# Hybrid encoder on one core: the projection phase's background work put out by a VectorE time budget, one chain step per block

## The chip, the cores and the metric

One Trainium2 chip, one core of it. The time is device microseconds of one execution. A median of three runs is given for the kernel before; the trace is of one further execution.

## The reference

One encoder layer and a last normalisation, for two request groups (prompt and sample) of 2048 tokens and 1024 channels each, with the same weights. One projection makes every branch's input:

```python
h = rmsnorm(x, norm_g)
p = h @ w_in
hy_u, hy_z, cf_a, cf_z, xa_q, xa_z = jnp.split(p, SPLITS, axis=-1)
k2 = hyena_two_sided_filter(L, ...)
y_hy = hyena_branch(hy_u, hy_short_w, hy_short_b, k2, hy_skip) * jax.nn.silu(hy_z)
y_cf = conformer_branch(cf_a, cf_dw_w, cf_dw_b, cf_ln_g, cf_ln_b) * jax.nn.silu(cf_z)
y_xa = memory_attention(xa_q, rmsnorm(mem, mem_norm_g), xa_w_kv) * jax.nn.silu(xa_z)
mix = jnp.concatenate([y_hy, y_cf, y_xa], axis=-1)
return x + mix @ w_out
```

`conformer_branch` is a gated value, a depthwise convolution of 31 taps over positions, a layer norm over 256 channels and a silu. `hyena_two_sided_filter` is three small layers with sines, an output matmul and a decay. `hyena_branch` is a convolution of width 3 on three projections, and a long convolution by Fourier transforms. All of it in float32.

## The kernel before

Matmuls of float32 data are made from three products of a high and a low part (`split`, L178 and L179: a cast on ScalarE, a subtraction on POOL or, for some, VectorE). The kernel has a **projection phase**, up to about 1381 us, then attention and the Fourier transforms, then the output phase. The change touches the first.

The projection has 26 weight columns of 128 channels for each of the two groups, and four token blocks of 512: 208 **blocks** of 24 matmuls (8 pieces of the depth, 3 products, L416 to L418, `proj`). Blocks 0 to 103 are group 0, 104 to 207 group 1. A block writes one of two PSUM banks (`pj`), and ScalarE's copy or activation, for Q also a VectorE subtraction (L522, L523), reads it and frees it. Column order in a group: CG and CV (gate and value of the conformer), ZC, then X1 and V in turn (blocks 24 to 55, in group 1 128 to 159), ZH and X0 in turn (56 to 87, 160 to 191), then ZX and Q. Blocks of X1, V and X0 pass the short convolution: a ScalarE copy (L430), POOL's middle tap (L437), VectorE's two others (L439, L441); V also a POOL product (L458).

In the shadow of these blocks runs **background** work, in two queues of closures, `bgq` and `fq`. After each block a number of closures is popped and run (L678): 7 a column from `bgq`, one from `fq`. What is run there is put into the program at that place; the Tile scheduler then orders each engine's instructions by a timeline of its own. The queues are filled at given columns (`QUEUE`, L628):

- the memory's keys and values (`kv_background`), after the first chunk of columns;
- the conformer's convolution for each group (`cf_background`): for each of four token blocks (b0 to b3 in group 0, b4 to b7 in group 1) a start on POOL, 60 taps on VectorE (L220: 30 more taps, two halves of the channels), then a chain: the mean of the two halves (POOL sum L226, split, two matmuls with a matrix of ones L228 and L229), subtraction (L235), squares (L240), their mean by the same lines, Sqrt (L242), reciprocal on VectorE (L245), a product and a silu (L249, L250), a product with the gate and the store (L256);
- the Hyena filter (`filter_background`, from block 102 on): for each of eight pieces three layers (`mlp`: matmul L295, VectorE L297, POOL, VectorE L303 three times, POOL, sine L306) and four times `taps` (matmuls L321 to L323, VectorE product L326, matmul L333, store);
- the first steps of the Fourier transforms of group 0 (`a_background`): load, transposes (L607), matmuls (L614 to L616).

What is left in the queues is put out behind the last block (`bg(len(fq), fq)`, `bg(len(bgq))`).

## Time and profile before

| what | value |
|---|---|
| median of three runs | 2147.4 us (2142.19 to 2153.81) |
| the profiled execution | 2152.26 us |
| its span | 2150.5 us |
| PE busy | 2008.1 us |
| VectorE busy | 1281.9 us |
| mean granted clock of TensorE | 0.978 |
| end of the projection phase | 1380.5 us |

The span is what the profiler saw from the first to the last instruction. A window row gives for a stretch the busy time of each engine with its count of instructions, and the granted TensorE clock (1.00 is 2.4 GHz, 0.50 is 1.2 GHz). A wait row tells which engine and line waited for which, in total, how often and the longest.

### The profile page before, as it was taken

What the parts mean: (1) busy time and instruction counts of PE and PEld (TensorE: products, weight loads), DVE (VectorE), ACT (ScalarE), POOL (GpSimd) and SP (SyncE); (2) the same over time, 40 slices, a digit from 0 to 9 for tenths busy, and PEclk for the clock granted to TensorE, in tenths of its full rate; (3) what the DMA queues carried; (4) which work ended last, traced back from release to release, by engine and by line L of the source; (5) the groups of instructions that cost most, each with busy time, mean ns of one, the idle gap of its engine ahead of it and who ended that gap; (6) DMA issues with size and microseconds to landing.
All of it is one profiled execution on the core that took longest, in us unless ns stands there. A gap on an engine that the chain in (4) does not pass through costs nothing.

```text
span 2150.5 us, 26677 instructions
## 1 busy us (share of the span) xinstructions
PE 2008.1 (93%) x9186; PEld 1603.0 (75%) x9186; DVE 1281.9 (60%) x1779; ACT 777.1 (36%) x1475; POOL 905.5 (42%) x861
## 2 busy tenths in 40 slices
PE   5999998987999999999999899999998789999998
PEld 4888876776787788877777678789733278888886
DVE  5756397978316363479495952277897724333443
ACT  5531212131424233232333243377787711111211
POOL 3434475655433111465554541365598811111110
PEclk8999999999999999999999999999999999999999
DMA  9643222331656332222222237799688776655552
GB/s 331 206 171 133 88 99 89 108 109 69 225 180 221 125 108 100 80 92 73 103 81 102 93 106 225 210 296 270 194 263 266 236 196 153 155 148 151 145 152 57
DMA packets 198306, 333.95 MB, mean 155 GB/s; under 512 B 53161, under 2 KB 74297, under 8 KB 195354
## 3 DMA queue, kind: packets, MB, share of 16 engines
q1 hardware_dynamic: 170938, 273.11, 41.0%
q10 hardware_dynamic: 21392, 46.18, 6.5%
q0 software_dynamic: 5840, 12.95, 2.2%
q8 instruction: 73, 1.20, 0.2%
q14 instruction: 63, 0.52, 0.1%
HBM read 200.50 MB, written 131.66 MB: 154 GB/s over the span
## 4 chain that ended last, share of the span: by engine, by line
PE 63%; DVE 16%; DMA 9%; issue 5%; POOL 3%; ACT 3%; SPq 1%; ACTq 0%; POOLq 0%; DVEq 0%
PE pj L417 11%; PE pj L418 11%; PE pj L416 11%; DVE bg L220 9%; PE ms L943 5%; PE ms L945 5%; PE ms L944 5%; PE tr L926 2%; PE po L767 2%; DVE sm L439 2%; DMA in<-xf 2%; PE pa L819 1%; DVE big L367 1%; PE ms L553 1%; PE ms L746 1%
## 5 line engine op out<-in xcount | busy, mean ns | idle before, releaser
L416 PE MATMUL pj<-xh,whi 128*128 128x512 f32 (+1 forms) x1728 | 672.0, 389 | 29.2 <-ACT xh L386 8.7
L417 PE MATMUL pj<-xl,whi 128*128 128x512 f32 (+1 forms) x1728 | 670.6, 388 | 8.0 <-POOL xl L387 6.7
L418 PE MATMUL pj<-xh,wlo 128*128 128x512 f32 (+1 forms) x1728 | 669.2, 387 | 0.0
L220 DVE SCALAR_TENSOR_TENSOR bg<-bg,vb,bg 128x512 f32<-128x512 f32 x480 | 418.0, 903 | 10.5 <-POOL bg L215 5.7
L416 PEld LDWEIGHTS pj<-xh,whi 128*128 128x128 f32 x1728 | 331.8, 192 | 99.4 <-ACT xh L386 9.6
L417 PEld LDWEIGHTS pj<-xl,whi 128*128 128x128 f32 x1728 | 332.1, 192 | 73.0 <-POOL xl L387 7.7
L418 PEld LDWEIGHTS pj<-xh,wlo 128*128 128x128 f32 x1728 | 332.3, 192 | 64.9 <-DMA wlo<-ws 0.4
L943 PE MATMUL ms<-wo,mh 128*128 128x512 f32 x512 | 205.9, 402 | 1.8 <-ACT mh L178 1.8
L944 PE MATMUL ms<-wo,mh 128*128 128x512 f32 x512 | 200.5, 392 | 0.0
L945 PE MATMUL ms<-wo,ml 128*128 128x512 f32 x512 | 198.4, 394 | 0.2 <-POOL ml L179 0.2
L439 DVE SCALAR_TENSOR_TENSOR sm<-sm,va,sm 128x448 f32<-128x448 f32 (+1 forms) x96 | 83.7, 871 | 162.7 <-POOL sm L437 133.4
L437 POOL TENSOR_SCALAR sm<-sm,va 128x448 f32<-128x448 f32 (+1 forms) x96 | 113.3, 1180 | 136.9 <-ACT sm L430 130.4
L458 POOL TENSOR_TENSOR big<-big,sm 128x448 f32<-128x448 f32 (+1 forms) x64 | 121.2, 1894 | 107.9 <-DVE sm L441 101.2
L946 DVE TENSOR_TENSOR xr<-xr,ms 128x512 f32<-128x512 f32 x64 | 44.0, 688 | 202.9 <-PE ms L945 202.9
L185 POOL TENSOR_TENSOR ss<-ss,mhalf 128x1 f32<-128x1 f32 x32 | 17.6, 550 | 315.9 <-DVE ss L184 315.9
L183 ACT ACTIVATE junk<-xr 128x1024 bf16<-128x1024 f32 x32 | 33.8, 1058 | 318.4 <-DVE xr L946 318.4
L430 ACT COPY sm<-pj 128x512 f32<-128x512 f32 x96 | 56.2, 585 | 213.9 <-PE pj L418 167.9
L179 POOL TENSOR_TENSOR wlo<-sm,whi 128x512 fp32r<-128x512 f32 x50 | 82.1, 1658 | 72.4 <-ACT whi L178 62.1
L943 PEld LDWEIGHTS ms<-wo,mh 128*128 128x128 f32 x512 | 96.8, 189 | 20.5 <-ACT mh L178 2.6
L945 PEld LDWEIGHTS ms<-wo,ml 128*128 128x128 f32 x512 | 96.1, 188 | 20.9 <-POOL ml L179 0.6
L944 PEld LDWEIGHTS ms<-wo,mh 128*128 128x128 f32 x512 | 96.7, 189 | 18.9
L758 POOL TENSOR_TENSOR ynp<-ynp,se 128x512 f32<-128x512 f32 x64 | 66.0, 1040 | 63.0 <-DVE se L756 53.7
(179 smaller groups left out, 3061.1 us busy)
## 6 DMA issues: line engine op xcount, KB each, us to landing
big<-in_xt_dram SPq DMA_DIRECT2D x32, 512.0 KB, 5.7
in<-x1d SPq DMA_DIRECT2D x128, 128.0 KB, 3.3
aa<-o ACTq DMA_DIRECT2D x64, 256.0 KB, 3.0
at<-aa SPq DMA_DIRECT2D x64, 256.0 KB, 4.1
out_dram<-xr ACTq DMA_DIRECT2D x64, 256.0 KB, 3.2
sm<-in_win_dram SPq DMA_DIRECT2D x52, 256.0 KB, 3.3
ws<-whi SPq DMA_DIRECT2D x52, 256.0 KB, 2.2
ws<-wlo SPq DMA_DIRECT2D x52, 256.0 KB, 4.1
```

The source lines that it names most:

```text
L179: (sub_eng or nc.gpsimd).tensor_tensor(lo, src, hi.bitcast(F32), op=ALU.subtract)
L220: nc.vector.scalar_tensor_tensor(st["a", c], st["h", c][:, k:k + TB], vb[:, 2 * k + c:2 * k + c + 1], st["a", c], op0=ALU.mult, op1=ALU.add)
L416: nc.tensor.matmul(ps[:, ts_], hi, xh[:, k, ts_], start=k == 0, stop=False)
L417: nc.tensor.matmul(ps[:, ts_], hi, xl[:, k, ts_], start=False, stop=False)
L418: nc.tensor.matmul(ps[:, ts_], lo, xh[:, k, ts_], start=False, stop=k == KC - 1)
L437: nc.gpsimd.tensor_scalar(ct[:, o:e], pt[:, o + 1:e + 1], w[1], va[:, 52 + ch:53 + ch], op0=ALU.mult, op1=ALU.add)
L439: nc.vector.scalar_tensor_tensor(ct[:, o:e], pt[:, o:e], w[0], ct[:, o:e], op0=ALU.mult, op1=ALU.add)
L458: nc.gpsimd.tensor_tensor(v, v, out, op=ALU.mult)
L758: nc.gpsimd.tensor_tensor(ev, ev, se.unsqueeze(2).broadcast_to([P, 2, 256]), op=ALU.mult)
L943: nc.tensor.matmul(po, mh[:, k, :], woh[k][:, hs], start=i == 0, stop=False)
L944: nc.tensor.matmul(po, mh[:, k, :], wol[k][:, hs], start=False, stop=False)
L945: nc.tensor.matmul(po, ml[:, k, :], woh[k][:, hs], start=False, stop=i == 7)
```

## The change

Every closure gets a cost in VectorE microseconds and a mark that says whether it belongs to a chain. After each block, `background(us)` gets a credit of 6.0 us less the VectorE time of the block's own column (2.2 for X0, X1 and V, 0.8 for CV and Q, 0.1 for others), and runs closures from `fq`, then `bgq`, while the credit is above zero. A marked closure runs only in a block in which its queue has put out nothing else.

```diff
-    LEAD, BR, FR, PF = 8, 7, 1.0, 0
+    LEAD, PF = 8, 0
...
-    def bg(n, q=bgq):
-        for _ in range(min(n, len(q))):
-            q.popleft()()
+    pace = {"block": 0, "credit": 0.0, "last": {id(bgq): -1, id(fq): -1}}
+
+    def background(us):
+
+        pace["block"] += 1
+        pace["credit"] = min(pace["credit"], us) + us
+        chained = set()
+        while pace["credit"] > 0:
+            for q in (fq, bgq):
+                if not q:
+                    continue
+                cost, chain, fn = q[0]
+                if chain and (id(q) in chained or pace["last"][id(q)] == pace["block"]):
+                    continue
+                if chain:
+                    chained.add(id(q))
+                q.popleft()
+                fn()
+                pace["last"][id(q)] = pace["block"]
+                pace["credit"] -= cost
+                break
+            else:
+                break
...
-                        background(BR * len(cs), FR)
+                        background(sum(6.0 - own(col) for col, _ in cs))
```

The conformer's chain is cut into other steps: the sum and its split (`total`); mean, subtraction, squares, their sum and split (`center`); the second mean, Sqrt, reciprocal and products (`var`); silu, gate and store (`outp`). Before they were mean with sum, split and subtraction; squares with sum, split and Sqrt; reciprocal; products and silus; gate and store, all by the rate of 7.

```diff
+            def halves(st, src, tmp):
+                st["hi"], st["lo"] = bt(TB, F32R), bt(TB, F32R)
                 nc.gpsimd.tensor_tensor(tmp, src[0], src[1], op=ALU.add)
-                split(hi, lo, tmp)
...
+                        bgq.append((0.9, False, lambda st=st, c=c, k=k: tap(st, c, k)))
+                bgq.append((0.5, True, lambda st=st: total(st)))
+                bgq.append((1.4, True, lambda st=st: center(st)))
+                bgq.append((3.4, True, lambda st=st: var(st)))
+                bgq.append((0.0, True, lambda st=st, b=b: (outp(st, b, 0), outp(st, b, 1))))
```

In the filter, the second matmul of `taps` (`spec`) comes one step later, and the layers of the next piece stand between the taps of this one:

```diff
-            for b in range(8):
-                st = {}
-                for ly in range(3):
-                    fq.append(lambda st=st, b=b, ly=ly: mlp(st, b, ly))
-                for n in range(4):
-                    fq.append(lambda st=st, b=b, n=n: taps(st, b, n))
+            for b in range(8):
                 for n in range(4):
+                    def step(b=b, n=n):
+                        if b or n:
+                            spec(b - (n == 0), (n - 1) % 4)
+                        taps(b, n)
+                        if b < 7 and n:
+                            mlp(st, b + 1, n - 1)
+                    fq.append((3.2 if b < 7 and n else 0.8, True, step))
```

The steps of keys and values and of `a_background` are marked as chains (costs 4.5, 1.3, 4.0 and 0.7); the two matmul steps after one transpose are one closure now.

Three places of the instruction order follow. PE around the first mean of token block b1 of the conformer, `ms` its PSUM tile, `pj` the block's; of before, where L228 is the mean's high part:

```order
L416 MATMUL pj_2815<-xh_786,whi_2520 128x512
L417 MATMUL pj_2815<-xl_787,whi_2520 128x512
L228 MATMUL ms_2602<-bg_2603,ones 128x512
L418 MATMUL pj_2815<-xh_786,wlo_2521 128x512
L416 MATMUL pj_2815<-xh_786,whi_2520 128x512
```

and of the change, where L256 and L257 are the two parts and L456 to L458 the block:

```order
L458 MATMUL pj_3018<-xh_608,wlo_2810 128x512
L256 MATMUL ms_3051<-bg_3013,ones 128x512
L257 MATMUL ms_3051<-bg_3014,ones 128x512
L456 MATMUL pj_3063<-xh_786,whi_2801 128x512
L457 MATMUL pj_3063<-xl_787,whi_2801 128x512
```

The mean stood within block 47, 17 matmuls in; it now stands between blocks 54 and 55, both parts together. PE at the end of block 200, in the change (b7, the last of group 1; L654 to L656 and L647 are matmuls and transposes of `a_background`):

```order
L458 MATMUL pj_9498<-xh_4816,wlo_9364 128x512
L256 MATMUL ms_9135<-bg_9097,ones 128x512
L257 MATMUL ms_9135<-bg_9098,ones 128x512
L256 MATMUL ms_9182<-bg_9142,ones 128x512
L257 MATMUL ms_9182<-bg_9143,ones 128x512
L654 MATMUL ms_9442<-bg_9405,big_9356 128x512
L655 MATMUL ms_9442<-bg_9405,big_9356 128x512
```

Both means of b7 stand back to back there, and nine more rows of `a_background` follow before block 201; before, the first mean stood behind block 191 and the second 14 matmuls into block 193. VectorE around the reciprocal of b7, before:

```order
L235 TENSOR_TENSOR bg_7675<-bg_7675,ms_8158 128x512
L439 SCALAR_TENSOR_TENSOR sm_9191<-sm_9187,va,sm_9191 128x576
L303 SCALAR_TENSOR_TENSOR f_8107<-f_8062,f_8107 128x256
L441 SCALAR_TENSOR_TENSOR sm_9191<-sm_9187,va,sm_9191 128x576
L303 SCALAR_TENSOR_TENSOR f_8107<-f_8062,f_8107 128x256 x2
L245 RECIPROCAL bg_7669<-bg_7669 128x512
L326 TENSOR_TENSOR f_8186<-ms_8182,f_8186 128x512
```

and in the change (L266 is the subtraction, L275 the reciprocal, L658 and L204 a copy and a split of `a_background`, L563 the subtraction that reads Q's PSUM bank, here of block 199):

```order
L266 TENSOR_TENSOR bg_8702<-bg_8702,ms_9135 128x512
L266 TENSOR_TENSOR bg_8706<-bg_8706,ms_9135 128x512
L204 TENSOR_TENSOR bg_9406<-tr_9400,bg_9405 128x512
L275 RECIPROCAL bg_8700<-bg_8700 128x512
L658 COPY sm_9446<-ms_9442 128x512
L204 TENSOR_TENSOR bg_9495<-tr_9489,bg_9494 128x512
L563 SCALAR_TENSOR_TENSOR sm_9482<-pj_9456,sm_9481 128x512
```

Before, the reciprocal was followed by the filter's product; now a read of a projection bank comes after it.

## Rows read from the trace of the kernel before

**Rows 1.** Page: busy us (share of the span) and instructions of each engine.

```profile
PE 2008.1 (93%) x9186; PEld 1603.0 (75%) x9186; DVE 1281.9 (60%) x1779; ACT 777.1 (36%) x1475; POOL 905.5 (42%) x861
```

**Rows 2.** Windows: length, busy us (count) of each engine, PE clock, DMA share, GB/s.

```profile
162.00:216.00 54.00, 54.00 (x240) 44.74 (x239) 33.64 (x41) 9.86 (x17) 24.60 (x13) 1.00 0.35 128
664.00:1381.00 717.00, 691.37 (x2962) 554.86 (x2960) 426.98 (x568) 234.61 (x331) 276.12 (x297) 0.99 0.35 116
343.30:353.50 10.20, 5.97 (x14) 4.71 (x15) 5.95 (x7) 1.69 (x3) 8.17 (x10) 0.50 0.07 27
978.20:985.00 6.80, 5.83 (x12) 3.91 (x13) 6.80 (x11) 1.63 (x2) 0.00 (x0) 0.50 0.12 41
```

**Rows 3.** PE's waits, 300 to 600 us: total us, times, longest us.

```profile
PE ms L228 <- ACT bg L178: 23.7, 3, 9.2
```

**Rows 4.** PE's waits, 664 to 1381 us.

```profile
PE ms L295 <- ACT f L306: 7.9, 4, 4.2
PE ms L333 <- DVE f L326: 6.9, 2, 3.6
...
PE ms L321 <- ACT big L178: 2.4, 1, 2.4
PE ms L323 <- POOL big L179: 1.7, 2, 1.5
```

**Rows 5.** Windows, group 0: second mean of a token block to the next first mean.

```profile
259.90:347.50 87.60, 75.39 (x318) 61.12 (x316) 85.28 (x87) 16.00 (x25) 56.96 (x49) 0.94 0.26 90
361.80:441.80 80.00, 69.74 (x299) 56.80 (x297) 72.06 (x77) 17.77 (x25) 43.87 (x36) 0.96 0.31 106
454.40:531.70 77.30, 65.84 (x290) 53.83 (x288) 69.00 (x73) 18.37 (x24) 44.66 (x33) 0.97 0.30 109
```

**Rows 6.** Lines on VectorE, 97 to 1381 us: busy us, mean ns | idle before.

```profile
L439 DVE SCALAR_TENSOR_TENSOR sm<-sm,va,sm 128x448 f32<-128x448 f32 (+1 forms) x96 | 83.7, 871 | 162.7 <-POOL sm L437 133.4 <-POOL sm L427 29.3
...
L303 DVE SCALAR_TENSOR_TENSOR f<-f,f 128x256 f32<-128x256 f32 x72 | 45.6, 633 | 16.0 <-POOL f L301 15.2
...
L245 DVE RECIPROCAL bg<-bg 128x512 f32<-128x512 f32 x8 | 26.8, 3352 | 23.3 <-ACT bg L242 23.3
...
L235 DVE TENSOR_TENSOR bg<-bg,ms 128x512 f32<-128x512 f32 x16 | 10.3, 683 | 10.2 <-PE ms L229 10.2
```

**Rows 7.** Timeline, 341 to 354 us: start us, us, engine, line [idle before].

```profile
345.13 1.70 POOL L226 TENSOR_TENSOR bg<-bg,bg 128x512 f32<-128x512 f32 x1
...
347.53 0.79 PE L228 MATMUL ms<-bg,ones 128*128 128x512 f32 x1 [7.27 <-ACT bg L178]
```

**Rows 8.** Windows, group 1: three runs of taps, first tap to last.

```profile
951.80:1028.30 76.50, 70.43 (x288) 55.33 (x287) 75.51 (x92) 16.84 (x27) 47.44 (x40) 0.96 0.25 89
1078.20:1142.50 64.30, 59.92 (x255) 48.50 (x254) 63.80 (x83) 22.39 (x27) 34.05 (x29) 0.97 0.28 95
1184.30:1248.70 64.40, 58.64 (x243) 45.84 (x242) 63.45 (x80) 18.91 (x25) 28.70 (x24) 0.97 0.31 100
```

**Rows 9.** Timelines of VectorE and POOL, from 157 and from 1010 us.

```profile
159.86 4.72 DVE L220 SCALAR_TENSOR_TENSOR bg<-bg,vb,bg 128x512 f32<-128x512 f32 x7
...
1018.80 2.30 DVE L220 SCALAR_TENSOR_TENSOR bg<-bg,vb,bg 128x512 f32<-128x512 f32 x1
...
1018.63 1.93 POOL L458 TENSOR_TENSOR big<-big,sm 128x576 f32<-128x576 f32 x1 [2.42 <-DVE sm L441]
```

**Rows 10.** Lines on ScalarE and POOL, 97 to 1381 us, by form.

```profile
L242 ACT ACT_TABLE_LOAD x8 | 10.3, 1283 | 7.8 <-PE ms L229 7.8
...
L240 ACT ACTIVATE bg<-bg 128x512 f32<-128x512 f32 x16 | 9.7, 631 | 11.0 <-DVE bg L235 11.0
...
L242 ACT ACTIVATE bg<-ms,eps 128x512 f32<-128x512 f32 x8 | 5.5, 689 | 0.1
...
L226 POOL TENSOR_TENSOR bg<-bg,bg 128x512 f32<-128x512 f32 x16 | 22.6, 1411 | 58.6 <-DVE bg L220 51.1 <-ACT bg L240 7.5
L179 POOL TENSOR_TENSOR bg<-bg,bg 128x512 fp32r<-128x512 f32 x16 | 21.0, 1315 | 10.7 <-ACT bg L178 10.7
```

More of the change, by code (lines that the diff above doesn't have):

```diff
@@ L222, in tap, with mean, total @@
                     op0=ALU.mult, op1=ALU.add)
-            def mean(src, tmp):
-                mp, hi, lo = ms(), bt(TB, F32R), bt(TB, F32R)
+            def halves(st, src, tmp):
+                st["hi"], st["lo"] = bt(TB, F32R), bt(TB, F32R)
                 nc.gpsimd.tensor_tensor(tmp, src[0], src[1], op=ALU.add)
-                split(hi, lo, tmp)
-                nc.tensor.matmul(mp, ones, hi, start=True, stop=False)
-                nc.tensor.matmul(mp, ones, lo, start=False, stop=True)
-                return mp
+                split(st["hi"], st["lo"], tmp)
+            def mean(st):
+                mp = ms()
+                nc.tensor.matmul(mp, ones, st["hi"], start=True, stop=False)
+                nc.tensor.matmul(mp, ones, st["lo"], start=False, stop=True)
+                return mp
+            def total(st):
+                halves(st, [st["a", c] for c in range(2)], st["h", 0][:, 0:TB])
             def center(st):
-                mp = mean([st["a", c] for c in range(2)], st["h", 0][:, 0:TB])
+                mp = mean(st)
                 for c in range(2):
                     nc.vector.tensor_tensor(st["a", c], st["a", c], mp, op=ALU.subtract)
-            def var(st):
                 for c in range(2):
@@ L619, in mult @@
                 nc.sync.dma_start(X1[2 * (n0 + i) + s, 0:128, :], xo)
[L621 removed]
+            bgq.append((0.0, False, load))
             for i in range(2):
[L623 to L625 removed]
+                bgq.append((0.7, True, lambda i=i: trans(i)))
+                bgq.append((0.7, True, lambda i=i: (mult(i, 0), mult(i, 1))))
         QUEUE = {(0, 0): [kv_background], (0, 4): [lambda: cf_background(0)], (1, 0): [filter_background],
```

69 lines of the change are left out of this document (34 added, 35 removed).

## Prediction

> **What bounds the kernel now.** I read the page first. TensorE (PE) is busy 93% of the span and no other engine more than 60% [rows 1], so the time can only fall where PE idles or runs at its lower clock. I then read the stretches. A stretch of the projection in which nothing disturbs PE issues 240 matmuls in 54.0 us [rows 2]: 0.225 us each by the count, 0.227 us where I follow starts, so a block of 24 takes 5.45 us. That is the yardstick below. The reader should see next that the same view has PE at 691 of 717 us from 664 us to the end of the projection, and that it issues only 14 matmuls, at half clock, in 10.2 us around 347 us [rows 2]. The rest of the loss is in the waits.
>
> Two chains make them. In group 0, "PE ms L228 <- ACT bg L178" is 23.7 us in three waits, up to 9.2 us [rows 3]: the first mean matmul of a conformer block waits for the split of the taps' sum. In group 1 the filter makes them: L295 waits for the sine (7.9 us), L333 for VectorE's L326 (6.9), L321 for ScalarE's split (2.4) [rows 4]; with L323's 1.7 that is 18.9 us. Each of three of them is followed by a stretch at half clock, the longest 6.8 us [rows 2], 13.6 us in all, which costs half of it: about 25.7 us together.
>
> Why the mean is late is in the windows from the second mean of one token block to the first mean of the next [rows 5]. In the first 87.6 us pass while PE issues 318 matmuls, worth 318 x 0.227 = 72.2 us: 15.4 us are lost. The second loses 80.0 - 67.9 = 12.1, the third 77.3 - 65.8 = 11.5 us. Together 39.0 us, and VectorE is busy 85.3 of 87.6 us in the first. So in these places VectorE's run of 60 taps is the longest thing, and PE's order decides how long it may take.
>
> **What the run needs.** From the second mean to the next first tap I take 7.3 us: Sqrt with its table load, then the reciprocal, 3.35 us [rows 6]. From the last tap to the mean 2.5 us: POOL starts the sum at 345.13 and PE the matmul at 347.53 [rows 7]. So 9.8 us lie outside the run. Inside it stand 60 taps and other VectorE instructions, mostly of the short convolution at about 0.85 us (L439 0.871 [rows 6]). In group 0, VectorE counts 87, 77 and 73 instructions [rows 5], less 60 taps, two subtractions and a reciprocal: 24, 14 and 10 others. That leaves (87.6 - 9.8 - 20.4) / 60 = 0.96 us a tap, then 0.97 and 0.98. In group 1 the runs themselves are listed [rows 8]: (76.5 - 32 x 0.85) / 60 = 0.82, (64.3 - 23 x 0.85) / 60 = 0.75, (64.4 - 20 x 0.85) / 60 = 0.79; I use 0.80. In rows where POOL is quiet seven taps take 4.72 us, 0.67 each; one tap beside a POOL multiply of 1.93 us takes 2.30 [rows 9].
>
> **The change, part by part.** The instructions are nearly the same; what moves is their place.
>
> *Conformer chain, group 0.* The means now stand 322, 277 and 291 matmuls behind the mean before (the first counted to the start of the block that the split holds up), worth 73.1, 62.9 and 66.1 us. The first run has the same 24 others, so it needs the 87.6 us of before and 0.6 for the eviction that ScalarE now has behind the split: 88.2 - 73.1 = 15.1 us late. The second has 8 others where 14 stood: 80.0 - 6 x 0.85 = 74.9, 12.0 late. The third has 12 for 10: 79.0, 12.9 late. Against that, the reciprocal of the last two no longer stands behind an eviction that ends after the mean; that is worth nothing or up to 3.4 us each by the length of the reciprocal [rows 6]. I take about 3: 9 and 10 us. So 34 us for 39: **-5** (bounds +1 and -12, the latter if the taps keep 0.90).
>
> *Filter.* One layer of the small net now follows the other after 41 to 49 matmuls, 9.3 to 11 us, with the product of the block before between them, and taps and their second matmul stand some 5 us apart. A layer is four VectorE instructions (L303, three of them, takes 0.63 us [rows 6]), three POOL steps and a sine, one behind the other. Before, a layer stood as far from the next, and its longest wait was 4.2 us, but taps and their product stood directly behind each other [rows 4]. Now those have room, and so has a layer where VectorE is not full, in the blocks of CG, CV and ZC; the waits beside X1/V blocks stay: I take 25.7 to about 7. **-19** (bounds -25 and 0).
>
> *Conformer chain, group 1.* Before, the filter spread over these blocks gave the means so much room that none waits. The filter now ends at block 162 and the next means stand 278, 274 and 257 matmuls after the ones before: 63.1, 62.2 and 58.4 us. Need, with 10 and 8 others: 60 x 0.80 + 8.5 + 9.8 = 66.3 and 64.6. So 3.2 and 2.4 us late, and some 3 of half clock: **+9** (bounds 0 and +29, the latter at 0.97 a tap). The last run lies where the weights are Z and Q columns and POOL is quiet; at 0.70 a tap it needs 42 + 6 + 9.8 = 57.8 and arrives in time.
>
> *The end of that chain.* In the new order PE has both means of the last token block directly behind block 200, and the split of block 199, which frees the PSUM bank of block 201, stands on VectorE behind the reciprocal. So PE stands through the chain: two means at two matmuls each 0.9, two subtractions 2 x 0.68, square 0.63, POOL sum 1.41, its split 0.63 (as long as the square) and 1.32, table load 1.28, Sqrt 0.69, reciprocal 3.35, then a copy, a small split and the split of Q at about 0.7 each, as long as a subtraction: 14 us [rows 6, 10]. 14 matmuls of a_background fill 14 x 0.227 = 3.2 of it, and the clock falls for some 2: **+13** (bounds 0, if the steps before it are early enough to let the scheduler's place not matter, and +18).
>
> *Behind the last block.* Three pieces of a_background and 30 PE instructions now come after the last projection matmul. Their PE time is the same as before; only their waits are new, each a ScalarE and a VectorE split of 0.6 to 0.7 us, as long as the square and a subtraction [rows 6, 10]. Four loads of the next stage also stand later on POOL's queue. **+3** (bounds 0 and +8).
>
> Nothing else is worth a term: the SyncE queue is in the same order, the memory's keys and values are put out over blocks 10 to 18 where the PE has no idle, and the attention and output stages differ in a few rows.
>
> **Sum.** -5 - 19 + 9 + 13 + 3 = +1 us. The profiled execution took 2152.3 us, 4.9 above the median of the three runs, so 2153 for it and **2148** by the median. Under 0.5%, 10.7 us, a measurement of this kernel cannot tell from no change.
>
> **Rivals.** *The budget works as a cap on VectorE.* If fewer taps are put out beside the blocks that load VectorE and POOL most, taps may take group 1's 0.80 us also in group 0: 3 x 60 x 0.17 = 31 of the 34 us go, and about 7 us of half clock with them: 2148 - 38 = **2110**. For it: 0.80 is measured, with POOL less busy (24.7 of 64 us there against 57 of 88 [rows 5, 8]). Against: in the new order the runs still follow the reciprocal directly, and the first has as many others as before.
>
> *Group 1's taps become as slow as group 0's.* This one is slower. The place is the two runs that now have no slack, from the means of blocks 163 and 177. At 0.97 us a tap they take 2 x 60 x 0.17 = 20 us more, all on PE: **2168**. It decides from 0.88 us a tap on (9.7 us above the forecast). For it: the X blocks bring L437 and L458 to POOL, and [rows 9] show what one tap pays beside L458. Against: group 1 measured 0.75 to 0.82 with filter work on POOL besides, which is now gone from there.
>
> The Trainium skill, "SBUF — State Buffer", section "Who interferes with whom", says that a VectorE instruction with two inputs in SBUF and a GpSimd instruction that reads SBUF exclude each other, the later one blocking until the first is done. By that rule a budget in VectorE time alone, with a fixed price for a tap, puts out too many taps in X blocks. The trace agrees: 2.30 us beside 1.93 us of L458, 0.67 alone.
>
> *The filter's waits stay.* VectorE may be just as full where the interleaved filter runs, since taps, a layer and the short convolution now share each block. Then the -19 falls away: **2167**. Against: no layer follows another closer than 9.3 us.
>
> **How the numbers follow.** The forecast has 0.52, the cap 0.25, slow taps 0.13, filter waits 0.10. The forecast's own range is 2134 to 2163 by its bounds taken half; of its 0.52 about 0.11 lie below -10.7 us and 0.08 above. Faster: 0.25 + 0.11 = 0.36. Slower: 0.08 + 0.11 + 0.08 = 0.27. Same: 0.37. The range goes from 2108, a little below the cap, to 2170, a little above both slower rivals.
>
> **What would show it.** Right: about 34 us of loss at three means in group 0; filter waits under 10 us; PE idle over 10 us once between the ends of blocks 200 and 201, ended by VectorE's split of Q; taps at 0.8 us in group 1. Wrong: no long wait behind block 200; waits for the split of the taps' sum under 10 us in all; or a tap mean in group 1 near that of group 0.

## The result: 0.9% slower, and where the time went

The changed kernel takes 2173.5 us in the median of seven runs (2167.65 to 2176.18). The kernel before took 2153.8 us in seven runs, among them the three from which the forecast started (median 2147.4). The ratio is 1.009, with an interval from 1.0069 to 1.011. The forecast was 2148 us, 1 us for the change; the measured time lies 3.5 us above the end of the range. The median of the kernel before makes 6.4 us of that distance, and the change itself cost 19.7 us.

The page of the changed kernel, span and busy row (it answers to [rows 1]):

```profile
span 2171.4 us, 26674 instructions
...
PE 2021.3 (93%) x9186; PEld 1610.8 (74%) x9186; DVE 1267.9 (58%) x1779; ACT 795.6 (37%) x1488; POOL 904.2 (42%) x861
```

TensorE (PE) is busy 13 us longer with the same 9186 matmuls, so more of them ran at half clock, and the rest of the 21 us is idle time. To see where, I cut both executions at the same blocks: 24, 88, 104 and 196, and at the last projection matmul. First the kernel before, windows with length, busy time of each engine (count), granted clock, DMA share and GB/s:

```profile
201.80:605.90 404.10, 367.48 (x1553) 298.97 (x1553) 279.21 (x305) 104.77 (x173) 232.34 (x208) 0.95 0.33 115
605.90:703.70 97.80, 92.74 (x420) 76.29 (x419) 43.58 (x87) 31.49 (x56) 30.40 (x22) 1.00 0.65 208
703.70:1296.30 592.60, 570.93 (x2420) 456.82 (x2419) 382.59 (x493) 193.35 (x264) 246.18 (x272) 0.99 0.28 96
1296.30:1380.50 84.20, 84.20 (x383) 68.78 (x382) 16.73 (x25) 22.81 (x38) 12.42 (x15) 1.00 0.69 213
1380.50:2150.50 770.00, 720.08 (x3507) 551.33 (x3505) 432.32 (x645) 338.57 (x763) 306.76 (x281) 0.98 0.69 194
```

and the same five stretches of the changed kernel:

```profile
202.10:604.10 402.00, 364.89 (x1553) 298.15 (x1552) 295.46 (x317) 95.46 (x144) 252.03 (x207) 0.95 0.30 106
604.10:712.30 108.20, 97.64 (x420) 78.92 (x420) 47.53 (x103) 41.66 (x86) 35.28 (x25) 0.95 0.71 226
712.30:1295.70 583.40, 569.95 (x2427) 457.60 (x2426) 345.35 (x453) 209.79 (x275) 226.67 (x265) 0.99 0.29 98
1295.70:1385.90 90.20, 81.33 (x345) 65.22 (x344) 43.58 (x61) 20.84 (x33) 16.68 (x16) 0.94 0.59 175
1385.90:2171.40 785.50, 733.48 (x3536) 558.94 (x3534) 434.00 (x651) 342.50 (x770) 309.73 (x287) 0.97 0.68 192
```

| stretch | before, us | after, us | difference |
|---|---|---|---|
| up to block 24 | 201.8 | 202.1 | +0.3 |
| blocks 24 to 88 (conformer of group 0) | 404.1 | 402.0 | -2.1 |
| blocks 88 to 104 (end of group 0) | 97.8 | 108.2 | +10.4 |
| blocks 104 to 196 (filter, conformer of group 1) | 592.6 | 583.4 | -9.2 |
| block 196 to the last projection matmul | 84.2 | 90.2 | +6.0 |
| behind it, to the end of the span | 770.0 | 785.5 | +15.5 |

The last row is the surprise. Part of it is plain: before the attention's first matmul, 6.4 us of a_background now run (L647 and L654 to L656: 30 of its 80 PE instructions), where before the attention began at once. The other 9.1 us are in the stage behind. The wait row of PE from 1381 to 1420 us:

```profile
PE tr L832 <- DMA u<-uu: 7.5, 1, 7.5
```

and POOL's timeline there, start and length in us:

```profile
1387.60 1.28 POOL L204 TENSOR_TENSOR big<-big,big 128x512 fp32r<-128x512 f32 x1 [12.26 <-ACT big L203]
1395.69 1.04 POOL L796 TENSOR_TENSOR ynp<-ynp,se 128x512 f32<-128x512 f32 x1 [6.81 <-DVE se L794]
1397.31 1.04 POOL L796 TENSOR_TENSOR ynp<-ynp,se 128x512 f32<-128x512 f32 x1 [0.57 <-DVE se L794]
1398.29 0.72 POOL L763 DMA_DIRECT2D wo<-qs  x1
1399.01 3.05 POOL L200 DMA_DIRECT2D u<-uu  x4
```

Before, the four loads of u were issued at 1371.9 us, nine us ahead of the last projection matmul; now at 1399.0. The reader should see the row at 1387.60: it is the split of the last piece of a_background. Two products of the attention (L796) and the loads stand behind it on POOL. It ended at 1388.9 us, and POOL then stood 6.81 us for the attention's own reciprocal (L794): the loads are late because these two products now stand ahead of them. PE's clock fell before PE's wait for u, behind one of 2.1 us, and is at half from 1395.8 to 1412.9 us.

Nearly all of the 15.5 us is lost at the start of that stage. The attention's 64th score matmul starts 51.3 us after the last projection matmul, before 36.7 us, which is 14.6 us later.

Blocks 88 to 104 are the second surprise. The loads of the second group's input, in the kernel before and in the changed one (shortest, median and longest issue, first and last start):

```profile
L354 SPq DMA_DIRECT2D bg<-in_x_sample_dram x32: 327/380/1248, 545.3 to 664.7; - x32
```

```profile
L394 SPq DMA_DIRECT2D bg<-in_x_sample_dram x32: 327/333/927, 583.6 to 673.8; - x32
```

They begin 38 us later, and ScalarE takes their squares between the evictions of these blocks. What PE waits for from 604 to 713 us:

```profile
PE pj L456 <- DVE sm L563: 7.2, 5, 4.0
PE pj L456 <- ACT sm L555: 2.5, 2, 2.3
```

In group 0 the waits are those of [rows 3], with one of 7.9 us moved to an eviction (L470) that ScalarE has behind its split of the taps' sum. The other two of L470 (3.8 and 1.9 us) do not come from that split: there ScalarE itself waited, last for a weight's low part on POOL and for the short convolution. Such waits stood there before as well (L430, 5.5 us):

```profile
PE ms L256 <- ACT bg L203: 17.6, 2, 9.5
PE pj L456 <- ACT sm L470: 13.6, 3, 7.9
PE pj L456 <- DVE bg L245: 4.3, 1, 4.3
```

In group 1 the filter's four rows of [rows 4] are gone altogether; the means wait instead:

```profile
PE ms L256 <- ACT bg L203: 10.8, 3, 5.8
PE pj L456 <- DVE sm L563: 5.3, 2, 3.5
PE pj L456 <- ACT big L521: 4.5, 1, 4.5
```

Three of these waits have other places and causes. 4.0 us of the first row lie behind block 200. 3.5 us of the second stand before block 198, where VectorE has Q's split behind sixteen taps. The 4.5 us are no mean's either: ScalarE stood before this eviction with the cast of a_background's table, waiting for its load:

```profile
1245.80 0.62 ACT L203 CAST big<-big 128x512 fp32r<-128x512 f32 x1 [12.50 <-DMA big<-in_t_dram]
```

### The profile page after: what moved, and what is told of

Read it like the earlier page. It is cut to its first block, busy times and chain, and to the rows that moved or that the text cites. A ratio compares the mean times of both kernels' runs of the same rounds, so it can differ in the third digit from the quotient of the medians.

```text
span 2171.4 us, 26674 instructions
## 1 busy us (share of the span) xinstructions
PE 2021.3 (93%) x9186; PEld 1610.8 (74%) x9186; DVE 1267.9 (58%) x1779; ACT 795.6 (37%) x1488; POOL 904.2 (42%) x861
## 4 chain that ended last, share of the span: by engine, by line
PE 60%; DVE 14%; DMA 10%; issue 7%; POOL 5%; ACT 3%; SPq 1%; ACTq 0%; POOLq 0%; DVEq 0%
PE pj L457 10%; PE pj L456 10%; PE pj L458 10%; DVE bg L245 8%; PE ms L981 5%; PE ms L983 5%; PE ms L982 5%; PE tr L964 2%; DMA bg<-in_x_sample_dram 2%; PE po L805 2%; DVE big L407 1%; PE tr L799 1%; PE ms L366 1%; DMA u<-uu 1%; DMA big<-in_xt_dram 1%
## 5 line engine op out<-in xcount | busy, mean ns | idle before, releaser
L456 PE MATMUL pj<-xh,whi 128*128 128x512 f32 (+1 forms) x1728 | 676.0, 392 | 48.6 <-ACT sm L470 14.5
L458 PE MATMUL pj<-xh,wlo 128*128 128x512 f32 (+1 forms) x1728 | 672.2, 389 | 0.0
L456 PEld LDWEIGHTS pj<-xh,whi 128*128 128x128 f32 x1728 | 333.5, 193 | 121.4 <-ACT sm L470 16.2
L458 PEld LDWEIGHTS pj<-xh,wlo 128*128 128x128 f32 x1728 | 334.1, 193 | 66.4 <-issue 1.2
L477 POOL TENSOR_SCALAR sm<-sm,va 128x448 f32<-128x448 f32 (+1 forms) x96 | 126.3, 1316 | 115.5 <-ACT sm L470 94.9
L479 DVE SCALAR_TENSOR_TENSOR sm<-sm,va,sm 128x448 f32<-128x448 f32 (+1 forms) x96 | 78.6, 818 | 143.8 <-POOL sm L477 113.9
L470 ACT COPY sm<-pj 128x512 f32<-128x512 f32 x96 | 56.2, 586 | 243.4 <-PE pj L458 175.1
L981 PEld LDWEIGHTS ms<-wo,mh 128*128 128x128 f32 x512 | 97.4, 190 | 21.0 <-ACT mh L203 2.8
L204 POOL TENSOR_TENSOR wlo<-sm,whi 128x512 fp32r<-128x512 f32 x50 | 72.1, 1450 | 55.2 <-ACT whi L203 49.7
L855 POOL TENSOR_TENSOR z<-z,us 128x512 f32<-128x512 f32 x64 | 80.8, 1275 | 21.8 <-DVE us L854 21.5
```

Source lines behind the costliest of these rows:

```text
L204: (sub_eng or nc.gpsimd).tensor_tensor(lo, src, hi.bitcast(F32), op=ALU.subtract)
L456: nc.tensor.matmul(ps[:, ts_], hi, xh[:, k, ts_], start=k == 0, stop=False)
L458: nc.tensor.matmul(ps[:, ts_], lo, xh[:, k, ts_], start=False, stop=k == KC - 1)
L477: nc.gpsimd.tensor_scalar(ct[:, o:e], pt[:, o + 1:e + 1], w[1], va[:, 52 + ch:53 + ch], op0=ALU.mult, op1=ALU.add)
L479: nc.vector.scalar_tensor_tensor(ct[:, o:e], pt[:, o:e], w[0], ct[:, o:e], op0=ALU.mult, op1=ALU.add)
L855: nc.gpsimd.tensor_tensor(z, z, us, op=op)
```

## The experiments

Each kernel was timed beside the kernel before; the changed kernel itself stands at 1.009. The kernel before had medians of 2151.5 to 2155.1 us on these occasions, so kernels of different occasions are compared by their ratios; with intervals like these, two ratios less than 0.003 (6 us) apart are not told from each other. Stretches are those of the table, from one execution. Where nothing near them was edited they repeat within a few us: behind the last matmul 782.6 to 787.2 us (experiments 2, 4, 6 and 9, which leave the same 30 instructions there). All kernels but the third start from the changed one.

**1. All of a_background before the last block.**

```diff
-                bgq.append((0.7, True, lambda i=i: trans(i)))
-                bgq.append((0.7, True, lambda i=i: (mult(i, 0), mult(i, 1))))
+                bgq.append((0.7, False, lambda i=i: trans(i)))
+                bgq.append((0.7, False, lambda i=i: (mult(i, 0), mult(i, 1))))
```

> The change, with the pieces of a_background no longer marked as chain steps, so that all of them are put out before the last block. Theory (the end of the projection): 15 of the 21 us lost lie between the last projection matmul and the attention, where a_background's rest runs 6 us and the next stage's u loads, queued behind it on POOL, come 7.5 us late. Then the time from the last projection matmul to the end goes back from 786 to about 771 us, the projection itself grows by about 4 us, and the whole falls by 9 to 14 us against the change. Rival (the work only moves back into the blocks, and the means of the last token block still hold the engine up): the whole falls by less than 4 us.

The whole rose: 2182.0 us, ratio 1.0143 (1.0123 to 1.0163). The theory was right about the end and wrong about the price. Behind the last matmul 767.3 us remain, 18 fewer. But from block 196 to the last matmul it takes 119.0 us for 90.2, because all pieces now stand at one place of PE's order, directly behind the means of the last token block, one waiting for the other. PE's waits there (1294 to 1370 us):

```profile
PE ms L256 <- ACT bg L203: 12.0, 2, 8.0
PE pj L456 <- DVE sm L563: 4.8, 2, 3.3
PE tr L647 <- DMA big<-uu: 3.5, 1, 3.5
PE ms L654 <- ACT big L203: 3.3, 1, 3.3
```

So the loss at the end hangs on where a_background stands, and it needs blocks between its steps to be hidden.

**2. Other tiles for the squares.** The edit takes in every input's squares, group 0's and the memory's too, not the second group's alone.

```diff
-                sq.append(bt())
+                sq.append(bt() if j < 2 else ft())
```

> The change, with two of the four tiles in which the inputs of the second group are squared taken from the filter's pool instead of the conformer's. Theory (buffers): in the change the conformer of group 0 ends 38 us later (first load of the second group's input at 583.6 us, before at 545.3) and holds the tiles these loads need, so ScalarE waits for them in blocks 88 to 104, which take 108.2 us for 97.8; with other tiles the first loads come before 570 us and the 16 blocks lose 5 to 10 of those 10 us. Rival (the loads are late because of the SyncE queue or DMA rate): the blocks stay above 106 us.

Blocks 88 to 104 took 96.4 us for 108.2, so the stretch is back at its time before (97.8). The first load into the conformer's tiles still came at 588.7 us, so "before 570 us" was wrong; it is the later loads that no longer queue. The whole is 2170.2 us, ratio 1.009 (1.0072 to 1.0109), no better: block 24 begins 6 us later, and the end stays at 787 us. The scheduler now hoists four of these loads to the start of the program, but that need not be what delays block 24: experiment 7, for the second group alone, has four of them there too and begins block 24 at 203.9 us.

**3. The filter's new order alone, in the kernel before.** The queue's rate and everything else stay.

```diff
+                    def step(b=b, n=n):
+                        if b or n:
+                            spec(b - (n == 0), (n - 1) % 4)
+                        taps(b, n)
+                        if b < 7 and n:
+                            mlp(st, b + 1, n - 1)
+                    fq.append(step)
```

> The kernel before, with only the filter's new order (layers of the next piece between the taps, second matmul of the taps a step later), one step a block as before. Theory (the filter part alone is a gain that the rest gives back): the waits for the filter, 18.9 us, fall below 5 us, and the whole falls by 12 to 22 us against the kernel before. Rival (the filter's waits are only moved to VectorE's full stretches, or its gain came from the budget): the whole changes by less than 6 us.

2151.8 us against 2152.1, ratio 0.9999 (0.9983 to 1.0014): the rival. The filter's waits fell from 18.9 to 7.7 us (0.7 of it in rows not shown), but the means, which had not waited once in group 1, now do (664 to 1381 us):

```profile
PE ms L228 <- ACT bg L178: 10.6, 2, 6.1
PE ms L295 <- ACT f L306: 3.9, 3, 2.8
...
PE ms L325 <- POOL big L179: 1.7, 1, 1.7
PE ms L323 <- ACT big L178: 1.4, 1, 1.4
```

The filter's matmuls stand behind blocks 102 to 198 in the kernel before and behind 102 to 167 here. So I read its spread as the slack that the conformer had: drawn together, it leaves the runs of taps to follow each other without room.

**4. The steps of the conformer's chain not kept apart.** The same for `center`, `var` and `outp`:

```diff
-                bgq.append((0.5, True, lambda st=st: total(st)))
+                bgq.append((0.5, False, lambda st=st: total(st)))
```

> The change, with the four steps of the conformer's chain not marked, so that they may be put out in one block. Theory (the separation of steps is not what costs or gains: the scheduler places the means by its own timeline, and they move by a block at most): within 6 us of the change. Rival (the separation is what makes the means late or early): more than 8 us either way, with the waits for the sum's split of group 0 changed by as much.

2167.9 us, ratio 1.0078 (1.0058 to 1.0097), not told from the change: as expected, the separation is not what costs. The scheduler puts the means almost where they were.

**5. u loaded from the SyncE queue.**

```diff
-            q = nc.gpsimd if n < LEAD + 2 else nc.sync
+            q = nc.sync
```

> The change, with the next stage's loads of u issued on the SyncE queue instead of POOL's. Theory (the loads are late because they stand on POOL behind the last split of a_background and two products of the attention): the wait of the first transpose on u, 7.5 us, goes, the half clock behind it shrinks, and the stretch from the last projection matmul to the end falls from 786 to 774 to 779 us; the whole falls by 7 to 11 us against the change. Rival (the loads wait for a_background's tiles or for the DMA engines, whichever queue issues them): the wait stays above 5 us and the whole within 3 us.

2166.8 us, ratio 1.0063 (1.0041 to 1.0085): 5.8 us less by the ratios, between the 7 that were expected and the rival's 3. Of L832's two waits for u (12.0 us up to 1480 us, 7.5 and 4.5) the first is gone and the second is longer (1381 to 1480 us):

```profile
PE tr L832 <- DMA u<-uu: 6.9, 1, 6.9
```

The 64th score matmul starts 6.5 us earlier, at 44.8 us behind the last projection matmul, but the stretch fell only to 783.4 us, no lower than in kernels that leave u on POOL (782.6 to 787.2). What the queue wins at the start of the stage is given back in it.

**6. A cheaper tap in the budget.**

```diff
-                        bgq.append((0.9, False, lambda st=st, c=c, k=k: tap(st, c, k)))
+                        bgq.append((0.65, False, lambda st=st, c=c, k=k: tap(st, c, k)))
```

> The change, with a tap's price in the budget 0.65 us instead of 0.9, so that more taps go out per block. Theory (late conformer, held tiles): the means of group 0 stand 3 to 4 blocks earlier, so the engine waits longer at them (5 to 12 us more in blocks 24 to 88), the inputs of the second group load earlier, and blocks 88 to 104 take 98 to 102 us for 108.2; the whole within 5 us of the change. Rival (the price of the tap is what makes the change slow): 10 us or more faster than the change.

2164.9 us, ratio 1.0062 (1.0038 to 1.0085). This supports experiment 2 from the other side. With the same tiles, but the conformer of group 0 done earlier, the loads begin at 558.5 us and blocks 88 to 104 take 96.3:

```profile
L394 SPq DMA_DIRECT2D bg<-in_x_sample_dram x32: 327/392/1232, 558.5 to 664.2; - x32
```

Blocks 24 to 88 took 405.4 us, 3.4 more. The whole is 8.6 us under the change by the medians and 6 by the ratios, short of the rival's 10 and not clear of the 5 us expected.

**7. Both repairs.** `alt` is true for the second group only.

```diff
-                sq.append(bt())
+                sq.append(ft() if alt and j > 1 else bt())
...
-            q = nc.gpsimd if n < LEAD + 2 else nc.sync
+            q = nc.sync
```

> The change, with both of the last two edits that address a loss outside the conformer's waits: the second group's squares half in the filter's tiles (for the second group only), and u on the SyncE queue. Theory (the two losses are separate): blocks 88 to 104 below 99 us and the stretch behind the last projection matmul below 779 us; the whole 16 to 22 us faster than the change, so within 5 us of the kernel before. Rival (what is won at one place is waited for at the next): less than 10 us faster than the change.

2162.1 us, ratio 1.0048 (1.0032 to 1.0064): 11.4 us less than the change by the medians, 9 by the ratios, where 16 to 22 were expected and less than 10 by the rival. Blocks 88 to 104 took 97.4, as expected; behind the last matmul 784.0, which was not. So that stretch is late whatever queue u is on.

**8. And the means later.**

```diff
+                for _ in range(2):
+                    bgq.append((0.0, True, lambda: None))
                 bgq.append((0.5, True, lambda st=st: total(st)))
```

> As the run before it, and two empty chain steps between the last tap and the sum of each token block, so that the means of group 0 stand 2, 6 and 8 blocks later on TensorE. Theory (the waits for the sum's split come only from where TensorE's order puts the mean): these waits, about 26 us in group 0, fall below 8 us, blocks 24 to 88 take under 385 us for 402, and the whole is 12 to 22 us faster than the run before it, less some us for the conformer's later end. Rival (the taps then run later by as much): the waits stay above 18 us, or come back at block 88 and behind, and the whole is within 6 us of the run before it.

2158.3 us, ratio 1.0031 (1.0008 to 1.0054), 3.8 us less than experiment 7, where 12 to 22 were expected and less than 6 by the rival. Blocks 24 to 88 fell from 402.8 to 387.6 us. No mean waits any more in group 0. What is left are evictions; before three of them (6.3, 7.2 and 7.2 us of the 27.4) ScalarE has its split of the taps' sum (PE's waits, 300 to 620 us):

```profile
PE pj L458 <- ACT sm L472: 27.4, 7, 7.2
PE pj L458 <- ACT big L523: 5.3, 2, 2.7
```

So PE's order was one cause and ScalarE's order the other. Part of what was won was lost again from block 88 on (108.0 us for 97.4), which is what the rival had said.

**9. The sum rounded by POOL, alone.**

```diff
-                split(st["hi"], st["lo"], tmp)
+                nc.gpsimd.tensor_tensor(st["hi"], src[0], src[1], op=ALU.add)
+                nc.gpsimd.tensor_tensor(st["lo"], tmp, st["hi"].bitcast(F32), op=ALU.subtract)
```

> The change, with the high part of the taps' sum rounded by POOL (a second sum written in the rounded type) instead of ScalarE. Theory (of the three late means of group 0 the first holds TensorE up by ScalarE's queue: its split of the sum stands before a block's eviction, so the eviction waits for the taps; the other two hold it up by their own place on TensorE): the eviction wait of about 8 us at the first is gone and becomes a wait of the mean itself of 5 us or more, blocks 24 to 88 fall by 0 to 6 us, the whole is within 6 us of the change. Rival (ScalarE's split is the cause at all three): blocks 24 to 88 fall by more than 15 us.

2173.6 us, ratio 1.0089 (1.0062 to 1.0116): as expected, nothing. The first mean's eviction wait became the mean's own, and other evictions (L525) wait longer (300 to 604 us; L260 is the mean here, L474 the eviction):

```profile
PE ms L260 <- POOL bg L253: 18.2, 3, 8.6
PE pj L460 <- ACT big L525: 7.2, 2, 4.0
PE pj L460 <- ACT sm L474: 5.9, 2, 3.8
```

**10. a_background in the filter's queue, alone.** Three steps for each piece, split tiles from the evictions' pool.

```diff
+            fq.append((0.7, True, lambda: (load(), trans(0))))
+            fq.append((1.4, True, lambda: (mult(0, 0), mult(0, 1), trans(1))))
+            fq.append((0.7, True, lambda: (mult(1, 0), mult(1, 1))))
```

> The change, with a_background put into the filter's queue from block 196 on, in three chain steps for each piece and with its split tiles from another pool, so that it neither waits for the steps nor for the tiles of the last conformer block. Theory (the end of the phase is late because a_background stands behind the conformer's last chain in one queue): fewer than half of its matmuls remain behind the last block, the stretch from the last projection matmul to the end falls from 786 to 773 to 780 us, the projection is not over 4 us longer, and the whole falls by 5 to 12 us. Rival (its place does not matter, the stage behind is bound by its own transfers): the stretch stays above 782 us.

2175.8 us, ratio 1.0096 (1.0068 to 1.0124), no better, where 5 to 12 us were expected. Behind the last matmul stand 6 of a_background's 80 PE instructions for 30, and 777.3 us, 8 fewer, as expected. But from block 196 it takes 102.7 us, because the means of the last token block still stand behind block 199 and hold up what follows. This is experiment 1 in small.

**11 and 12. All of it, with two empty steps and with one.** Experiments 8, 9 and 10 together (u stays on POOL), and the second group's squares only in tiles of the filter and of the evictions.

```diff
-                sq.append(bt())
+                sq.append((ft() if j < 2 else sm()) if alt else bt())
```

> All of it together: two empty steps before the sum, the sum rounded by POOL, the second group's squares in tiles of the filter and of the evictions, a_background in the filter's queue. Theory (the losses are separate and each edit takes its own away): blocks 24 to 88 below 370 us for 402, blocks 88 to 104 below 100 us, the stretch behind the last matmul below 780 us; the whole 2120 to 2140 us, faster than the kernel before. Rival (VectorE and POOL are the bound, so a wait taken away comes back at the next reader): above 2148 us.

> The same with one empty step. Theory: the means stand 2 to 8 blocks earlier than with two, so 8 to 16 us of their waits come back, and 3 to 6 us are won where the second group begins; 2125 to 2148 us, a little slower than with two. Rival (the conformer's late end costs more than the waits): faster than with two by 5 us or more.

2160.8 us, ratio 1.0032 (1.0018 to 1.0046), and 2180.6 us, 1.012 (1.0088 to 1.0151). Both missed: the first came out where its rival was, above 2148 us, and the second far above its 2125 to 2148. With two empty steps the end took 772.6 us, as expected, and blocks 24 to 88 took 376.0 us, short of the 370 expected, but blocks 104 to 112 took 76.7 us for 47. There PE waits 15.2 us for the scaling of the second group's input (L410), whose first square tile is now the filter's. With one step, 391.5 us, 77.4 in the same eight blocks, and 99.8 us from block 196 to the last matmul for 87.4.

**13 to 15. The same with other tiles for the squares.** Half in the filter's and half in the conformer's; only in the conformer's, as in the kernel before; and two token blocks as in 11, two as in the kernel before. The first:

```diff
-                sq.append((ft() if j < 2 else sm()) if alt else bt())
+                sq.append(ft() if alt and j > 1 else bt())
```

> Two empty steps before the sum, the sum rounded by POOL, a_background in the filter's queue (as in the run that was near the kernel before), but the second group's squares half in the filter's tiles and half in the conformer's. Theory (that run had lost its gain only in blocks 104 to 112, 76.7 us for 47, where the last squares stood in tiles that the filter waits to use and the evictions hold): blocks 24 to 88 below 380 us, blocks 88 to 112 below 152 us, behind the last matmul below 778 us; the whole 2124 to 2142 us, faster than the kernel before by 0.5 to 1.3%. Rival (the late conformer pushes the loss to wherever the next tile is missing): blocks 88 to 112 above 165 us and the whole above 2148 us.

> The same with the second group's squares only in the conformer's tiles, as in the kernel before. Theory (tiles held by the last conformer block delay the second group): blocks 88 to 112 take 8 to 25 us more than in the run with two pools, and the whole is as much slower. Rival (the tiles are no matter once the means no longer hold TensorE up): within 4 us of it.

> The same with the first two token blocks' squares in tiles of the filter and the evictions and the last two's in the conformer's. Theory (the tiles of the evictions are handed out in program order, so loads into them start late): blocks 88 to 104 below 100 us and 104 to 112 between 47 and 60 us, the whole 2128 to 2150 us. Rival (it is the filter's tiles that block): blocks 104 to 112 stay above 65 us.

2135.5 us, ratio 0.9913 (0.9891 to 0.9935); 2140.1 us, 0.9932 (0.9907 to 0.9957); 2133.1 us, 0.990 (0.9878 to 0.9923). All three beat both kernels, the kernel before by 0.7 to 1.0%. The stretches of the first:

```profile
207.00:583.20 376.20, 359.57 (x1550) 294.27 (x1548) 288.17 (x301) 82.79 (x121) 239.71 (x195) 0.98 0.30 106
583.20:688.00 104.80, 95.61 (x416) 77.21 (x417) 58.39 (x104) 47.12 (x97) 49.58 (x38) 0.97 0.73 243
688.00:1272.20 584.20, 571.11 (x2434) 459.09 (x2433) 347.68 (x464) 219.01 (x284) 234.16 (x272) 0.99 0.29 99
1272.20:1360.70 88.50, 82.67 (x368) 66.98 (x367) 48.98 (x69) 23.31 (x38) 19.52 (x18) 0.98 0.64 193
1360.70:2132.00 771.30, 725.15 (x3512) 553.43 (x3511) 431.95 (x646) 339.10 (x764) 311.17 (x286) 0.98 0.69 194
```

against 402.0, 108.2, 583.4, 90.2 and 785.5 of the change. PE's waits in group 0 (300 to 604 us) are down to

```profile
PE pj L462 <- ACT sm L476: 8.6, 4, 4.2
PE pj L462 <- ACT big L527: 8.0, 4, 2.7
```

The reader should see where the gain lies. Against the kernel before it is 27 to 30 us in blocks 24 to 88. Blocks 88 to 104 take 104.8, 105.0 and 101.1 us in the three, nearly as long as in the change: group 0's last means stand behind blocks 90 and 92, later still. That loss is not mended, only outweighed. Among these three choices the tiles matter little: the times lie within 7 us, with intervals that overlap. They do matter between experiments 11 and 13, which differ in nothing else and lie 25 us apart. As 13 shares the filter's tiles with the squares too and takes 45.5 us in blocks 104 to 112, that sharing alone is not the cause; 15, with 11's tiles for two of four token blocks, takes 56.8. Which of the two pools holds 11 up is not shown.

**16 and 17. One edit of three left out.** First a_background back in the conformer's queue, then the rounding back on ScalarE (both with two empty steps and the conformer's tiles). The third, the empty steps, was not left out by itself.

> The change with two of the three edits of the fast version: two empty steps before the sum and the sum rounded by POOL, with a_background left in the conformer's queue. Theory (a_background's place is worth what lies behind the last matmul): blocks 24 to 88 below 380 us as in the fast version, behind the last matmul 783 to 790 us; the whole 8 to 18 us slower than the fast version without the squares' edit. Rival (a_background's place is no matter once the means are late): within 4 us of it.

> The change with two empty steps and a_background in the filter's queue, the sum rounded by ScalarE as in the change. Theory (with the means late enough for TensorE, ScalarE's split before an eviction is what is left of the wait): blocks 24 to 88 take 383 to 390 us, 7 to 13 us more than with POOL's rounding, ended by an eviction; the whole 6 to 14 us slower than the fast version without the squares' edit. Rival (POOL's rounding only moves the wait): within 4 us of it.

2146.5 us, ratio 0.997 (0.9953 to 0.9988), and 2155.1 us, 1.0014 (1.0 to 1.0028), for 0.9932 with all three. By the ratios that is 8 us, at the lower edge of what was expected, and 18 us, more than the 6 to 14. Without a_background's new place the stretch behind the last matmul is 796.0 us, the longest of all, as here the most of it is left over (46 of 80 instructions); from block 196 it takes 11 us less. Experiment 8 leaves as many, with u on the SyncE queue, and takes 786.7 us; its other edits differ, so this only suggests that u's queue counts when more is left over. PE's waits from 1350 to 1460 us:

```profile
PE tr L838 <- DMA u<-uu: 9.8, 2, 5.0
PE ms L790 <- DMA wo<-qs: 5.4, 1, 5.4
```

Without POOL's rounding the eviction waits are back (300 to 620 us), and blocks 24 to 88 take 388.1 us for 377.3:

```profile
PE pj L458 <- ACT sm L472: 27.4, 7, 7.1
```

## Why the prediction was wrong, point by point

| step of the forecast | forecast, us | measured, us | without moved PE work, us |
|---|---|---|---|
| conformer, group 0 | -5 | -2.1 | -2.1 |
| filter, and conformer of group 1 | -19 + 9 | -9.2 | -10.8 |
| end of the conformer's chain | +13 | +6.0 | +14.4 |
| behind the last block | +3 | +15.5 | +9.1 |
| "Nothing else is worth a term" | 0 | +10.7 | +10.7 |
| sum | +1 | +20.9 | +21.3 |

The last column is an estimate, and it is the one to hold against the forecast, whose terms are waits and half clock, with PE's own work unchanged. PE issues 345 instructions from block 196 to the last projection matmul for 383, which took 0.220 us each before; 7 more stand in the stretch ahead, and a_background takes 6.4 us behind. So the forecast failed in two steps: a term that it put at nothing (+10.7) and one that it made too small (+3 for +9.1).

*Conformer, group 0.* Right in kind: its end held by an eviction behind the split at the first mean, by the mean itself at the others. By the prediction's own yardstick (0.227 us a matmul) 19.8, 11.5 and 12.5 us are lost up to the three means, 44 in all, where it had 34 and the kernel before 39. The gain at the second and third, from the reciprocal's new place, did not come.

*Filter and group 1.* The sum came out, and the sizes did not: the filter's waits fell to nothing, not to 7 us, and the means cost more than 9. In experiment 3 the filter's waits fell by 11.2 us, the means' rose by 10.6, and the whole stayed. So the two terms are one there: the filter's gain is the conformer's loss. That they share VectorE's time is the reading, not tested by itself.

*End of the chain.* The size came out by luck. The step that failed in detail is "the split of block 199, which frees the PSUM bank of block 201, stands on VectorE behind the reciprocal". The timeline of PE, ScalarE and VectorE:

```profile
1329.28 0.50 PE L257 MATMUL ms<-bg,ones 128*128 128x512 f32 x1
1333.81 0.50 PE L256 MATMUL ms<-bg,ones 128*128 128x512 f32 x1 [4.03 <-ACT bg L203]
...
1341.79 0.50 PE L456 MATMUL pj<-xh,whi 128*128 128x512 f32 x1 [0.52 <-ACT sm L555]
...
1341.14 0.60 ACT L555 ACTIVATE sm<-pj 128x512 f32<-128x512 f32 x1
...
1337.75 3.35 DVE L275 RECIPROCAL bg<-bg 128x512 f32<-128x512 f32 x1 [1.02 <-ACT bg L274]
...
1342.16 0.68 DVE L563 SCALAR_TENSOR_TENSOR sm<-pj,sm 128x512 fp32r<-128x512 f32 x1
```

PE starts block 201 at 1341.79, before VectorE's split of Q at 1342.16, and behind ScalarE's eviction L555. PE idles 4.0 us for the split of the squares, 0.85 and 0.5 us, not "over 10 us once"; the 14 instructions of a_background ran meanwhile at half clock. "No long wait behind block 200" was the prediction's own sign of being wrong. From block 200 to 201 it takes 18.3 us, before 9.1. The rest was not forecast: the 3.5 us before block 198, with the half clock behind it, and a_background's steps between the last blocks.

*Behind the last block.* The step that failed is "only their waits are new, each a ScalarE and a VectorE split of 0.6 to 0.7 us", +3 with a bound of +8. PE's time for a_background was counted rightly; it only moved here. The waits were priced by two splits, and the stage behind loses 9.1 us: PE waits 12.0 us for u there, before 5.1, and 2.1 us for the first results of the attention, with half clock from 1395.8 to 1412.9 us. The experiments grade the whole stretch by what is left over of a_background's 80 instructions: with none 767 us (experiment 1), 770 (3 and the kernel before); with 6, 771 to 780 (10 to 15 and 17); with 30, 783 to 787; with 46, 787 (8) and 796 (16). The late loads of u, which the prediction had named, decide the start of the stage, but moving their queue alone (5) brought nothing back at its end that stands clear of the scatter. What gives it back is open.

*Nothing else.* The larger of the two failed steps: no term for blocks 88 to 104, which lost 10.4 us. The prediction had the means of group 0 seven blocks later and did not ask who waits for the tiles of the last of them. Experiments 2 and 6 show it: blocks 88 to 104 return to 96 us both with other tiles and with an earlier conformer. One reason given, that "the SyncE queue is in the same order", did not hold there either: the change issues the first loads of the second group's transposed input (564.2 us) ahead of the first squares' (583.6), the kernel before behind them (571.2 and 545.3).

*The rivals.* Slow taps in group 1 came in part. The two runs named, of 59.1 and 59.8 us with 10 and 8 others, give 0.84 and 0.88 us a tap by the rule of the prediction, for 0.80 in the forecast and 0.97 in the rival; the second stands at the value from which the rival was to decide. The 7 us that this makes (an estimate: 60 x 0.04 + 60 x 0.08) are hidden in the sum of the filter's row. The slower side came mainly from a place that no rival named. The budget as a cap did not come: group 0's three runs give 0.99, 0.93 and 0.97 us a tap, before 0.97, 0.93 and 0.97, and the reason given against it, that the runs follow the reciprocal directly, fits.

*The range.* Half of each bound, added up, reaches from 2129 to 2175 us, not from 2134 to 2163; the measured time lies inside the former. That would have been right for the wrong reason, as the terms above show.

## What to carry to other kernels

When background work is put out later, ask first who waits for its end: the tiles that its last step holds and the stage behind the phase cost 20 us here (26 with the work that only moved), while the rest of the change came out about even. In these traces a late result stalled every engine on which something else stood behind its reader: PE at the mean, ScalarE at the split ahead of an eviction. Moving one reader showed nothing (experiments 9 and 10 alone gained nothing) until the others were moved too; together with the empty steps they were worth 1.6% against the change. A budget for one engine doesn't see this; the order of the other engines around the chain's readers does. And when work moves from one stretch to another, count it out before you hold a stretch against its forecast.

## What the runs showed of the hardware that was not expected

Around the two waits before the first transposes of the next stage (2.1 us up to 1395.5, 7.5 us up to 1408.2) TensorE's granted clock stayed at its lower level, 1.2 GHz, from 1395.8 to 1412.9 us, 17.1 us in one piece, although the attention's small matmuls ran between them. Inside the blocks, where matmuls of full size came before and after, it was 10.2 us around single waits of 7.9 and 9.5 us, and 13.7 us around two of 4.3 and 8.1. In the kernel before the same stage began at the lower level too, from 1384.4 to 1391.2 us, although PE had waited no longer than 0.94 us at a time since its last projection matmul: it had issued 12 small matmuls (128x256) in the 4 us before. These are single stretches; whether the size of the matmuls or the waits between them made them long was not tested.
